# Scores of two heads issued as one group, with the gate products last and the retention scores set apart

## The chip, the cores and the metric

The kernel runs on one core of a Trainium2 chip. The metric is the device time of one launch in microseconds (us); lower is better. Engines are called as the profile calls them: PE is TensorE (matrix products), PEld its weight loads, DVE is VectorE, ACT is ScalarE, POOL is GpSimd, SP is the engine whose queue issues the loads from memory.

## What is computed

Two layers of a decoder over 256 tokens of width 1024. Each layer has a mixer with three groups of heads behind one input projection, then a feed-forward part (dense in the first layer, eight experts of which two are used per token in the second) and a gated embedding. The change touches the mixer alone. Cut to what matters:

```python
def causal_block_attention(q, k, v, scale, cum_logf=None):
    ...
        s = jnp.einsum('bhqd,bhkd->bhqk', q_i, k).astype(jnp.float32) * scale
        if cum_logf is not None:
            s = s + blk[2][..., :, None] - cum_logf[:, :, None, :]
        ...
        w = jax.nn.softmax(s, axis=-1).astype(v.dtype)
        return jnp.einsum('bhqk,bhkv->bhqv', w, v)

def hybrid_mixer(...):
    ...
    o = causal_block_attention(qa, ka, va, HEAD_DIM ** -0.5)
    ...
    o_b = causal_block_attention(split_heads(qb, FOX_HEADS), split_heads(kb, FOX_HEADS),
                                 split_heads(vb, FOX_HEADS), FOX_DIM ** -0.5, cum)
    ...
    o_c = retention_chunkwise(qr, kr, split_heads(vc, RET_HEADS))
```

The first call is differential attention (four pairs of heads), the second forgetting attention (four heads; `cum` is the running sum of the logarithms of the gates, which is added to the scores), the third retention (four heads, scores times a fixed decay). All heads have 64 columns.

## The kernel before, in words

In the mixer each weight block of `w_in` (1 MB) is loaded, split by ACT and DVE into a rounded part `whi` and a rest `wlo` (`Ring.unit`, L178 to L199), and multiplied with the split activations `xh`, `xl` in three products per 128 rows. `tok_chunks` (L313) gives results by token, `col_half` (L344) by column; `col_half` and the VC chunk are 48 products of 128x256 each. Results go through PSUM tiles `mm` (four) and `aux` (four).

Between these blocks stand the small products of the heads:

- `ret_scores(hd)` (L521): two fp32 products of 64 rows, `qkc` with itself, 256 and 128 columns, into one `aux`; DVE multiplies by `c_decay` into `at`.
- `fox_scores(hd)` (L480): `softmax_head` (L353) with `extra`. The queries and keys `qkb` of an even head lie in partitions 0 to 63, of an odd one in 64 to 127. The gates' sums stand in four rows for each head, in partitions from 32 times the head's number on (`row0`, `row1`, written by `fox_rows`, L448). For the first 128 queries and then for the second 128, a 64-row product of `qkb` is followed at once by a 4-row product of the rows, which adds to the same columns:

```python
for a, b, qs, ks in ((0, 128, slice(0, 128), slice(0, 128)), (128, 384, slice(128, 256), slice(0, 256))):
    mm(ps[:, a:b], q[:, qs], k[:, ks], True, extra is None)
    if extra is not None:
        mm(ps[:, a:b], extra[0][:, qs], extra[1][:, ks], False, True)
```

- `diff_scores(p)` (L410): the same helper without `extra`, for the two heads of pair p, on `qa` and `ka`.
- After the scores of a softmax head, DVE adds the mask and takes the row extremes (L363, `nz`, `nm`) and ACT takes the exponentials (L367, `e`).
- `fox_out(hd)` (L488): three transposes of `e` (`turn_w`, L374), a copy to `wt` by ACT (L376), three products with `vb`, and two scalings by DVE (L495). `ret_out()` (L533): twelve products of `at` and `vc`, then a normalisation over `oc` on ACT, DVE and POOL (L538 to L551).

In the trace an fp32 product of the heads leaves two records, one of the gates' rows (rounded type) one.

The order of these calls is written out at the end of `mixer` (L557 to L601); a scheduler of the tile library then places the instructions of each engine, so that blocks overlap a little. Each engine works through its own list in order. Both layers run the same mixer.

Of the kernel before, what the change touches and what calls it, by code (L numbers as in the profile page):

```python
# [11 lines left out]
FT = mybir.dt.float32  # L12
# [3 lines left out]
OP = mybir.AluOpType  # L16
# [19 lines left out]
QA, KA, VA, QB, KB, VB, FB, QC, KC, VC, GC, END = 0, 512, 1024, 1536, 1792, 2048, 2304, 2308, 2564, 2820, 3076, 3332  # L36
# [59 lines left out]
def hymba_trunk(ctx: ExitStack, tc: tile.TileContext, A: dict, out: bass.AP, stop=None, dump=None):  # L96
    nc = tc.nc
    V, G, ACT, PE = nc.vector, nc.gpsimd, nc.scalar, nc.tensor
# [4 lines left out]
    small = pool("small", 4)  # L103
# [3 lines left out]
    def mmtile():  # L107
        return psum.tile([128, 512], FT, name="mm", tag="mm")

    def aux():  # L110
        return psum.tile([128, 512], FT, name="aux", tag="aux")
# [89 lines left out]
    def mm(o, a, b, start, stop):  # L201
        return PE.matmul(o, a, b, start=start, stop=stop, skip_group_check=True)  # L202
# [16 lines left out]
    def tok_mm(o, x, ks, unit, n0, n, t, start, stop):  # L219

        r = slice(t * 128, (t + 1) * 128)
        return steps(o, unit, ks, lambda w, j: w[:, j, n0:n0 + n], x, r, True, start, stop)

    def col_mm(o, x, ks, unit, c0, start, stop):

        steps(o, unit, ks, lambda w, j: w[:, j, c0:c0 + 128], x, slice(0, S), False, start, stop)
# [78 lines left out]
    def mixer(i, ring, xp, xnp, mp, wk, first=None):  # L305
        win = A["w_in"][i]
        g = gain_0 if i == 0 else gain(A["norm_mix"][i])
        x, r = rows_turned(xp, xnp, g)
        r_row = scale_row(r, mp)
        lam_init = 0.8 - 0.6 * math.exp(-0.3 * i)  # L310
        K = {}

        def tok_chunks(*chunks):  # L313
            work = []
            for c0, n, evict in chunks:
                if n > 260:
                    us = [(ring.unit(win[kk * 512:(kk + 1) * 512, c0:c0 + n], 4, n), range(4 * kk, 4 * kk + 4))
                          for kk in range(2)]
                else:
                    src = first if first is not None and c0 == VB else win[:, c0:c0 + n]  # L320
                    us = [(ring.unit(src, 8, n), range(8))]
                work.append((n, evict, us))
                constants(c0)
            for t in range(NT):
                for n, evict, us in work:
                    ps = mmtile()
                    for j, (u, ks) in enumerate(us):
                        tok_mm(ps[:, :n], x, ks, u, 0, n, t, j == 0, j == len(us) - 1)
                    evict(t, ps)
# [14 lines left out]
        def col_half(c0, o, half):  # L344
            u = ring.unit(win[:, c0 + half * 256:c0 + half * 256 + 256], 8, 256)
            for j in range(2):
                ps = mmtile()
                col_mm(ps[:, :S], x, range(8), u, j * 128, True, True)
                V.tensor_tensor(o[:, 2 * half + j], ps[:, :S], r_row, op=OP.mult)

        otok = [xnp.tile([128, D], FT, name="xn", tag="xn") for t in range(NT)]

        def softmax_head(q, k, s, extra=None):  # L353

            ps = aux()
            for a, b, qs, ks in ((0, 128, slice(0, 128), slice(0, 128)), (128, 384, slice(128, 256), slice(0, 256))):
                mm(ps[:, a:b], q[:, qs], k[:, ks], True, extra is None)
                if extra is not None:
                    mm(ps[:, a:b], extra[0][:, qs], extra[1][:, ks], False, True)
            nz = wk.tile([128, 384], FT, name="nz")  # L360
            nm = small.tile([128, 2], FT, name="nm")
            for j, (a, b) in enumerate(((0, 128), (128, 384))):
                V.tensor_tensor_reduce(nz[:, a:b], ps[:, a:b], K["mask"][:, a:b], scale=-0.125, scalar=3e38,  # L363
                                       op0=OP.add, op1=OP.min, accum_out=nm[:, j:j + 1])
            e = wk.tile([128, 384], FT, name="e", bufs=6)
            for j, (a, b) in enumerate(((0, 128), (128, 384))):
                ACT.activation(e[:, a:b], nz[:, a:b], AF.Exp, bias=nm[:, j:j + 1], scale=-1.0,  # L367
                               accum_out=s[:, j:j + 1])
            return e
# [18 lines left out]
        qa = mp.tile([128, 4, S], FT, name="qa")  # L388
        ka = mp.tile([128, 4, S], FT, name="ka")
# [19 lines left out]

        def diff_scores(p):  # L410
            s = small.tile([128, 4], FT, name="ds")
            es = []
            for j in range(2):
                r = slice(64 * j, 64 * j + 64)
                es.append(softmax_head(qa[r, p], ka[r, p], s[:, 2 * j:2 * j + 2]))
            V.reciprocal(s, s)
            V.tensor_scalar(s[:, 2:4], s[:, 2:4], K["nlam"], None, op0=OP.mult)
            w = es[1]
            for j, (a, b) in enumerate(((0, 128), (128, 384))):
                V.tensor_scalar(w[:, a:b], w[:, a:b], s[:, 2 + j:3 + j], None, op0=OP.mult)  # L420
                V.scalar_tensor_tensor(w[:, a:b], es[0][:, a:b], s[:, j:j + 1], w[:, a:b], op0=OP.mult,
                                       op1=OP.add)
            K["w", p] = w
# [18 lines left out]
        qkb = mp.tile([128, 4, S], FT, name="qkb")  # L442
# [34 lines left out]
                V.scalar_tensor_tensor(row, ps[:, :S], K["crow"][:, z:z + 1], rt, op0=OP.add, op1=OP.subtract)  # L477
                K["row", z] = row

        def fox_scores(hd):  # L480
            r = slice(64 * (hd % 2), 64 * (hd % 2) + 64)
            rr = slice(32 * hd, 32 * hd + 4)
            s = small.tile([128, 2], FT, name="fs", bufs=4)
            e = softmax_head(qkb[r, hd // 2], qkb[r, 2 + hd // 2], s, (K["row", 0][rr], K["row", 1][rr]))
            V.reciprocal(s, s)
            K["e", hd] = e, s

        def fox_out(hd):  # L488
            e, s = K.pop(("e", hd))
            wt = turn_w(e)  # L490
            ps = aux()
            o = ps[:, :128].rearrange("p (t n) -> p t n", t=NT)
            av(o, wt, vb, hd * 64, 64)
            for t in range(NT):
                V.tensor_scalar(otok[t][:, 512 + hd * 64:576 + hd * 64], o[:, t], s[:, t:t + 1], None, op0=OP.mult)  # L495
# [3 lines left out]
        vc = mp.tile([128, NT, 256], FT, name="vc")  # L499
# [21 lines left out]
        def ret_scores(hd):  # L521
            dec = K["decay"].rearrange("p (h n) -> p h n", h=4)
            r = slice(64 * (hd % 2), 64 * (hd % 2) + 64)
            q, k = qkc[r, hd // 2], qkc[r, 2 + hd // 2]
            ps = aux()
            mm(ps[:, :256], k[:, :128], q, True, True)
            mm(ps[:, 256:384], k[:, 128:], q[:, 128:], True, True)
            at = wk.tile([128, 384], FT, name="at", bufs=4)
            V.tensor_tensor(at[:, :256], ps[:, :256], dec[:, hd], op=OP.mult)
            V.tensor_tensor(at[:, 256:], ps[:, 256:384], dec[:, hd, :128], op=OP.mult)  # L530
            K["at", hd] = at

        def ret_out():  # L533
            po = aux()
            po_v = po.rearrange("p (t h n) -> p t h n", t=NT, h=4)
            for hd in range(4):
                av(po_v[:, :, hd], K.pop(("at", hd)), vc, hd * 64, 64)
            ACT.copy(oc, po.rearrange("p (g n) -> p g n", n=64))  # L538
            mu = small.tile([128, 8], FT, name="mu", bufs=1)
            V.tensor_reduce(mu, oc, axis=mybir.AxisListType.X, op=OP.add)  # L540
            V.scalar_tensor_tensor(oc, mu[:, :, None].to_broadcast([128, 8, 64]), -1.0 / 64, oc, op0=OP.mult,
                                   op1=OP.add)
            sq = wk.tile([128, 2, 4, 64], FT, name="rot_b", bufs=1).rearrange("p w h d -> p (w h) d")
            ACT.activation(sq, oc, AF.Square)
            va8 = small.tile([128, 8], FT, name="va8", bufs=1)
            V.tensor_reduce(va8, sq, axis=mybir.AxisListType.X, op=OP.add)
            rv = rsqrt_mean(va8, 8, 1.0 / 64)
            V.tensor_tensor(oc, oc, rv[:, :8, None].to_broadcast([128, 8, 64]), op=OP.mult)
            for t in range(NT):
                o = oc[:, 4 * t:4 * t + 4].rearrange("p g n -> p (g n)")  # L550
                V.tensor_tensor(o, o, K["rgn"], op=OP.mult)  # L551
# [6 lines left out]
        tok_chunks((VB, 260, vb_evict), (QC, 512, rotate))  # L558
        fox_rows()
        col_half(QB, qkb, 0)  # L560
        col_half(QB, qkb, 1)
        ret_scores(0)
        ret_scores(1)
        fox_scores(0)
        fox_scores(1)
        tok_chunks((VC, 256, lambda t, ps: V.tensor_scalar(vc[:, t], ps[:, :256], r[t], None, op0=OP.mult)))
        ret_scores(2)
        ret_scores(3)
        fox_scores(2)
        fox_scores(3)  # L570
        col_half(QA, qa, 0)
        fox_out(0)
        fox_out(1)
        ret_out()
        col_half(KA, ka, 0)
        fox_out(2)
        fox_out(3)
        diff_scores(0)
# [658 lines left out]
```

## Time and profile before

| what | value |
|---|---|
| runs | 1496.1, 1492.35 and 1498.77 us, median 1496.1 |
| the profiled execution: its own time | 1499.37 us |
| its span, first to last instruction | 1497.6 us |
| mean granted TensorE clock | 0.988 |
| DVE, ACT busy, share of the span | 80%, 67% |
| loaded from memory | 439.77 MB |

The span lies 1.8 us under the execution's own time. The first layer's mixer runs from the start to about 130 us, the second's from about 365 to 490 us; the experts take most of what follows. A share of busy time is a mean over such stages. Of the clock, 1.00 stands for 2.4 GHz and a fall to 0.5 for 1.2 GHz; a window's clock is a mean over it.

### The profile page before, as it was taken

The numbers are of one execution on the slowest core, as the hardware profiler recorded it, in microseconds if no ns is written. First come the engines' busy times: TensorE is split into PE (matmuls) and PEld (weight loads), VectorE is DVE, ScalarE is ACT, GpSimd is POOL, SyncE is SP. The second block draws the span as 40 slices with busy tenths as digits, with TensorE's granted clock in tenths as the row PEclk, the third lists the DMA queues.
The fourth block names the chain that finished last, engine by engine and source line by source line (L and its number), as shares of the span: only waits on it lengthen the run. The fifth ranks groups of instructions, "written<-read, shape, count | busy, mean of one in ns | idle before, by whom it ended". The sixth has DMA issues, their size and how long they took to land. (4 is left out here: it accounts for less than half of the span.)

```text
span 1497.6 us, 20501 instructions
## 1 busy us (share of the span) xinstructions
PE 1462.2 (98%) x7778; PEld 1228.8 (82%) x7778; DVE 1192.0 (80%) x1209; ACT 1005.1 (67%) x1061; POOL 31.4 (2%) x73
## 2 busy tenths in 40 slices
PE   8999999999999999999999999999999999999997
PEld 7987999997897888887788877888877878888876
DVE  6576555557666687999997999997999998889875
ACT  5455444447546576787976787975787976676756
POOL 0001000001000100000000000000000000000001
PEclk9899999999999999999999999999999999999998
DMA  9634555645624799999998999999999999899940
GB/s 295 174 129 140 182 187 180 196 169 175 205 95 155 275 349 348 355 397 372 407 409 331 378 400 374 403 408 350 379 379 397 397 409 394 317 390 328 387 167 30
DMA packets 166429, 442.25 MB, mean 295 GB/s; under 512 B 13489, under 2 KB 56753, under 8 KB 166322
## 3 DMA queue, kind: packets, MB, share of 16 engines
q1 hardware_dynamic: 166322, 440.85, 79.6%
q8 instruction: 63, 1.03, 0.3%
q14 instruction: 44, 0.36, 0.1%
HBM read 439.77 MB, written 1.05 MB: 294 GB/s over the span
## 5 line engine op out<-in xcount | busy, mean ns | idle before, releaser
L190 DVE TENSOR_TENSOR wlo<-raw,whi 128x2048 fp32r<-128x2048 f32 (+2 forms) x474 | 920.5, 1978 | 146.7 <-ACT whi L189 141.3
L189 ACT CAST whi<-raw 128x2048 fp32r<-128x2048 f32 (+2 forms) x474 | 771.5, 1662 | 254.6 <-PE mm L202 148.3
L202 PE MATMUL mm<-whi,xgh 128*128 128x512 f32 x560 | 222.4, 397 | 0.0
L202 PE MATMUL mm<-whi,xgl 128*128 128x512 f32 x560 | 219.3, 392 | 0.0
L202 PE MATMUL mm<-wlo,xgh 128*128 128x512 f32 x560 | 154.0, 396 | 0.0
L202 PE MATMUL mm<-xh,whi 128*128 128x256 f32 x512 | 131.2, 288 | 0.0
L202 PE MATMUL mm<-xl,whi 128*128 128x256 f32 x512 | 129.9, 286 | 0.0
L202 PEld LDWEIGHTS mm<-whi,xgh 128*128 128x128 f32 x560 | 105.1, 188 | 24.8
L202 PEld LDWEIGHTS mm<-whi,xgl 128*128 128x128 f32 x560 | 105.3, 188 | 22.6
L202 PEld LDWEIGHTS mm<-wlo,xgh 128*128 128x128 f32 x560 | 103.5, 188 | 22.5
L202 PE MATMUL mm<-whi,xh 128*128 128x512 f32 (+2 forms) x328 | 111.6, 355 | 2.3 <-ACT xh L229 2.3
L202 PE MATMUL mm<-whi,xl 128*128 128x512 f32 (+2 forms) x328 | 112.0, 354 | 0.0
L202 PE MATMUL aux<-whi,hxh 128*128 128x512 f32 x280 | 110.4, 396 | 0.7 <-ACT hxh L229 0.7
L202 PE MATMUL aux<-whi,hxl 128*128 128x512 f32 x280 | 109.3, 392 | 0.0
L202 PEld LDWEIGHTS mm<-xh,whi 128*128 128x128 f32 x512 | 98.5, 192 | 1.5 <-issue 0.9
L202 PEld LDWEIGHTS mm<-xl,whi 128*128 128x128 f32 x512 | 98.9, 193 | 0.5
L202 PE MATMUL mm<-wlo,xgp 128*128 128x512 f32 x336 | 95.2, 405 | 1.1
L202 PE MATMUL mm<-whi,xgp 128*128 128x512 f32 x336 | 92.0, 395 | 0.3 <-ACT whi L189 0.2
L202 PE MATMUL mm<-wlo,xh 128*128 128x512 f32 (+2 forms) x328 | 88.8, 351 | 0.1
L202 PE MATMUL mm<-xh,wlo 128*128 128x256 f32 x512 | 83.2, 283 | 0.0
L202 PE MATMUL aux<-wlo,hxh 128*128 128x512 f32 x280 | 77.2, 397 | 0.4 <-DVE wlo L190 0.4
L202 PEld LDWEIGHTS mm<-wlo,xgp 128*128 128x128 f32 x336 | 60.0, 188 | 21.2 <-DVE wlo L190 10.3
(240 smaller groups left out, 1872.4 us busy)
## 6 DMA issues: line engine op xcount, KB each, us to landing
raw<-in_moe_w_gate_dram SPq DMA_DIRECT2D x112, 1024.0 KB, 7.3
raw<-in_moe_w_up_dram SPq DMA_DIRECT2D x112, 1024.0 KB, 7.7
raw<-in_moe_w_down_dram SPq DMA_DIRECT2D x110, 1024.0 KB, 8.0
raw<-in_w_in_dram SPq DMA_DIRECT2D x24, 1024.0 KB, 6.6
raw<-in_dense_w_gate_dram SPq DMA_DIRECT2D x11, 1024.0 KB, 5.4
raw<-in_dense_w_up_dram SPq DMA_DIRECT2D x11, 1024.0 KB, 5.3
raw<-in_dense_w_down_dram SPq DMA_DIRECT2D x11, 1024.0 KB, 5.0
raw<-in_w_out_dram SPq DMA_DIRECT2D x8, 1024.0 KB, 4.9
```

The source lines that it names most:

```text
L189: self.split = (ACT.copy(hi, v[:, k]), V.tensor_tensor(lo, v[:, k], hi.bitcast(FT), op=OP.subtract))
L190: V.tensor_tensor(lo, v[:, k], hi.bitcast(FT), op=OP.subtract))
L202: return PE.matmul(o, a, b, start=start, stop=stop, skip_group_check=True)
```

## The change

`softmax_head` is cut in two. A new `scores_pair` issues the 64-row products of two heads, first both heads' 128 columns and then both heads' 256, and only then, where there are gates, the four 4-row products of both heads. `start` is set on the first part of a tile alone. `fox_scores` now takes a pair of heads, `diff_scores` uses the same helper. The order of the calls changes: the retention's scores no longer stand next to the forgetting ones.

```diff
-        def softmax_head(q, k, s, extra=None):
-
-            ps = aux()
-            for a, b, qs, ks in ((0, 128, slice(0, 128), slice(0, 128)), (128, 384, slice(128, 256), slice(0, 256))):
-                mm(ps[:, a:b], q[:, qs], k[:, ks], True, extra is None)
-                if extra is not None:
-                    mm(ps[:, a:b], extra[0][:, qs], extra[1][:, ks], False, True)
+        PARTS = ((0, 128, slice(0, 128), slice(0, 128)), (128, 384, slice(128, 256), slice(0, 256)))
+
+        def scores_pair(q, k, extra=None):
+
+
+            pss = [aux() for j in range(2)]
+            for n, (a, b, qs, ks) in enumerate(PARTS):
+                for j in range(2):
+                    mm(pss[j][:, a:b], q(j)[:, qs], k(j)[:, ks], n == 0, extra is None)
+            if extra is not None:
+                for a, b, qs, ks in PARTS:
+                    for j in range(2):
+                        mm(pss[j][:, a:b], extra(j)[0][:, qs], extra(j)[1][:, ks], False, True)
+            return pss
+
+        def softmax_head(ps, s):
+
             nz = wk.tile([128, 384], FT, name="nz")
...
         col_half(QB, qkb, 0)
-        col_half(QB, qkb, 1)
         ret_scores(0)
         ret_scores(1)
+        col_half(QB, qkb, 1)
         fox_scores(0)
+        tok_chunks((VC, 256, lambda t, ps: V.tensor_scalar(vc[:, t], ps[:, :256], r[t], None, op0=OP.mult)))
         fox_scores(1)
-        tok_chunks((VC, 256, lambda t, ps: V.tensor_scalar(vc[:, t], ps[:, :256], r[t], None, op0=OP.mult)))
+        col_half(QA, qa, 0)
         ret_scores(2)
         ret_scores(3)
-        fox_scores(2)
-        fox_scores(3)
-        col_half(QA, qa, 0)
         fox_out(0)
         fox_out(1)
+        col_half(KA, ka, 0)
         ret_out()
-        col_half(KA, ka, 0)
         fox_out(2)
         fox_out(3)
         diff_scores(0)
```

On PE, at the first forgetting scores of layer 0, the list before reads as follows (`qkc` are retention products, `qkb` the forgetting heads' 64-row products, `row_379,row_369` the 4-row products of the gates, `mm` a weight block):

```order
L202 MATMUL aux<-qkc 128x256
L202 MATMUL aux<-qkc 128x128
L202 MATMUL aux<-qkc 128x256
L202 MATMUL aux<-qkc 128x128
L202 MATMUL aux<-qkb 128x128
L202 MATMUL aux<-row_379,row_369 128x128
L202 MATMUL aux<-qkb 128x256
L202 MATMUL aux<-row_379,row_369 128x256
L202 MATMUL aux<-qkb 128x128
L202 MATMUL aux<-row_379,row_369 128x128
L202 MATMUL aux<-qkb 128x256
L202 MATMUL aux<-row_379,row_369 128x256
```

And now, at the same scores:

```order
L202 MATMUL mm<-xl,whi 128x256
L202 MATMUL mm<-xh,wlo 128x256 x4
L202 MATMUL aux<-qkb 128x128 x2
L202 MATMUL aux<-qkb 128x256 x2
L202 MATMUL aux<-row_379,row_369 128x128 x2
L202 MATMUL aux<-row_379,row_369 128x256 x2
L202 MATMUL mm<-whi,xh 128x256
```

The seven changes between 64-row and 4-row products within a pair's list have become one, and weight-block products stand on both sides; the retention's four products moved to before the block that precedes these. The number of products is the same.

On ACT, from the end of the QA block to the first two forgetting outputs of layer 0 (`whi` is a weight split, `wt` the copy of the turned weights, `oc` the retention's output), before:

```order
L189 CAST whi<-raw 128x1024
L376 COPY wt<-aux 128x384
L189 CAST whi<-raw 128x1024
L376 COPY wt<-aux 128x384
L538 COPY oc<-aux 128x512
```

And now:

```order
L189 CAST whi<-raw 128x1024 x2
L386 COPY wt<-aux 128x384 x2
L189 CAST whi<-raw 128x1024 x2
L551 COPY oc<-aux 128x512
L386 COPY wt<-aux 128x384 x2
```

The first `wt` now stands behind two weight splits in place of one.

On DVE, from the retention's output to the scores of the first differential pair (`mu`, `va`, `oc` belong to the retention's normalisation, `xn` to the forgetting outputs, `nz,nm` to the differential scores), now:

```order
L553 TENSOR_REDUCE mu<-oc 128x8
L508 TENSOR_SCALAR xn<-aux,fs 128x64
L554 SCALAR_TENSOR_TENSOR oc<-mu,oc 128x512
L508 TENSOR_SCALAR xn<-aux,fs 128x64 x3
L559 TENSOR_REDUCE va_825<-rot_b 128x8
L373 ISA nz,nm<-aux,c_mask 128x128
L373 ISA nm 128x1
L373 ISA nz,nm<-aux,c_mask 128x256
L373 ISA nm 128x1
L561 TENSOR_TENSOR oc<-oc,rs_r 128x512
L373 ISA nz,nm<-aux,c_mask 128x128
```

Before, all the normalisation's instructions up to the products with `rgn` stood ahead of these `xn` and `nz`; now they are mixed with them, and the second head's `nz` stands behind `oc<-oc,rs_r`. The lists of POOL are unchanged, and on SP one load of a gain moved behind one load of weights.

## Rows read from the trace of the kernel before

**Rows 1.** The page: busy us, share of the span and instructions of each engine.

```profile
PE 1462.2 (98%) x7778; PEld 1228.8 (82%) x7778; DVE 1192.0 (80%) x1209; ACT 1005.1 (67%) x1061; POOL 31.4 (2%) x73
```

**Rows 2.** Busy time by stretch, mixer of layer 0: columns in its first line.

```profile
core 0: us, PE busy (x) PEld busy (x) DVE busy (x) ACT busy (x) POOL busy (x), PEclk, DMA share, GB/s
...
37.44:100.00 62.56, 62.43 (x433) 56.59 (x432) 38.82 (x109) 26.49 (x56) 1.85 (x2) 0.92 0.49 148
```

**Rows 3.** Waits of SP's queue from 500 us on: us in total, times, longest.

```profile
SPq L123 <- DVE wlo L190: 681.8, 304, 8.4
```

**Rows 4.** Timeline of PE, first forgetting scores, layer 0: start us, us, instruction.

```profile
42.90 0.63 PE L202 MATMUL mm<-xh,wlo 128*128 128x256 f32 x4
43.46 0.93 PE L202 MATMUL aux<-qkc 64*128 64x256 f32 x8
44.22 0.38 PE L202 MATMUL aux<-qkb 64*128 64x128 f32 x2
44.53 0.32 PE L202 MATMUL aux<-row,row 4*128 4x128 f32 x1
44.79 0.70 PE L202 MATMUL aux<-qkb 64*128 64x256 f32 x2
45.41 0.38 PE L202 MATMUL aux<-row,row 4*128 4x256 f32 x1
...
47.02 0.38 PE L202 MATMUL aux<-row,row 4*128 4x256 f32 x1
47.33 0.39 PE L202 MATMUL mm<-whi,xh 128*128 128x256 f32 x1
```

**Rows 5.** Timeline of PE, last forgetting outputs and first differential scores, layer 0.

```profile
78.27 0.49 PE L374 MATMUL aux<-ident,e 128*128 128x128 f32 x3
...
82.17 0.93 PE L202 MATMUL aux<-ka,qa 64*128 64x128 f32 x8
83.03 0.39 PE L202 MATMUL mm<-xh,wlo 128*128 128x256 f32 x1
```

**Rows 6.** Busy time by stretch around the forgetting scores of both layers.

```profile
47.30:51.20 3.90, 3.90 (x21) 3.88 (x21) 1.92 (x7) 1.38 (x6) 0.00 (x0) 0.57 0.52 150
...
55.50:58.90 3.40, 3.40 (x16) 1.89 (x12) 2.78 (x9) 1.79 (x5) 0.00 (x0) 0.88 0.00 0
58.90:65.00 6.10, 6.10 (x29) 6.09 (x29) 2.46 (x9) 1.04 (x5) 0.00 (x0) 0.51 0.52 153
...
403.10:406.20 3.10, 3.10 (x16) 1.82 (x13) 2.82 (x9) 2.77 (x5) 0.00 (x0) 1.00 0.18 67
406.20:409.70 3.50, 3.50 (x17) 3.48 (x17) 1.92 (x7) 1.38 (x6) 0.00 (x0) 0.51 0.17 16
...
414.40:417.50 3.10, 3.10 (x16) 1.82 (x12) 2.81 (x9) 1.49 (x4) 0.00 (x0) 1.00 0.00 0
417.50:423.00 5.50, 5.50 (x47) 5.48 (x47) 2.35 (x8) 1.37 (x6) 0.00 (x0) 1.00 0.46 127
```

**Rows 7.** Timeline of ACT, first forgetting output, layer 0.

```profile
67.15 1.05 ACT L189 CAST whi<-raw 128x1024 fp32r<-128x1024 f32 x1 [6.81 <-issue]
68.10 0.47 ACT L376 COPY wt<-aux 128x384 f32<-128x384 f32 x1
```

**Rows 8.** Timeline of PE, first forgetting output, layer 0.

```profile
67.37 0.49 PE L374 MATMUL aux<-ident,e 128*128 128x128 f32 x3
...
68.63 0.88 PE L202 MATMUL aux<-vb,wt 128*128 128x64 f32 x6
```

**Rows 9.** Timeline of DVE, the retention's normalisation, layer 0; in brackets the idle time before.

```profile
74.64 0.69 DVE L540 TENSOR_REDUCE mu<-oc 128x8 f32<-128x512 f32 x1 [2.82 <-ACT oc L538]
...
79.49 0.69 DVE L548 TENSOR_TENSOR oc<-oc,rs_r 128x512 f32<-128x512 f32 x1 [2.06 <-POOL rs_r L238]
80.21 0.76 DVE L551 TENSOR_TENSOR oc<-oc,rgn 128x256 f32<-128x256 f32 x2
```

**Rows 10.** Busy time by stretch, from the last forgetting outputs on, layer 0.

```profile
80.00:90.00 10.00, 9.97 (x84) 8.91 (x83) 9.20 (x30) 4.88 (x13) 0.00 (x0) 1.00 0.31 105
90.00:100.00 10.00, 10.00 (x63) 8.97 (x62) 6.41 (x17) 3.75 (x10) 0.00 (x0) 1.00 0.41 140
```

More of the change, by code (lines that the diff above doesn't have):

```diff
@@ L411, in diff_scores @@
             s = small.tile([128, 4], FT, name="ds")
[L412 to L415, printed above, removed]
+            r = [slice(64 * j, 64 * j + 64) for j in range(2)]
+            pss = scores_pair(lambda j: qa[r[j], p], lambda j: ka[r[j], p])
+            es = [softmax_head(pss[j], s[:, 2 * j:2 * j + 2]) for j in range(2)]
             V.reciprocal(s, s)
@@ L478, in fox_rows, with fox_scores @@
                 K["row", z] = row
[L480 to L486, printed above, removed]
+        def fox_scores(p):
+            r = [slice(64 * j, 64 * j + 64) for j in range(2)]
+            rr = [slice(32 * (2 * p + j), 32 * (2 * p + j) + 4) for j in range(2)]
+            pss = scores_pair(lambda j: qkb[r[j], p], lambda j: qkb[r[j], 2 + p],
+                              lambda j: (K["row", 0][rr[j]], K["row", 1][rr[j]]))
+            for j in range(2):
+                s = small.tile([128, 2], FT, name="fs", bufs=4)
+                e = softmax_head(pss[j], s)
+                V.reciprocal(s, s)
+                K["e", 2 * p + j] = e, s
         def fox_out(hd):
```

## The prediction

> **What bounds the kernel now.** I read the page first: PE is busy for 98% of the span [rows 1]. That alone says little, because matmuls overlap, so the stage that the change touches is read next. In the mixer of layer 0, PE is busy for 62.43 of 62.56 us while DVE, ACT and the DMA have large reserves [rows 2]. The mixer is bound by PE: what PE saves there, the stage saves, as long as nobody is late for it. The same view shows a granted clock of 0.92 in this stretch, which is the second thing to look at. The experts that follow are paced by SP's queue, which waits for a raw buffer that DVE's split gives back (681.8 us over 304 waits [rows 3]). Their loads start when the second mixer and the routing behind it are through, so an earlier mixer moves that stage as a whole. I take a microsecond of PE in either mixer as a microsecond of the run.
>
> **The forgetting scores.** There are four groups of a retention pair and a forgetting pair, two in each layer. The timeline of PE shows one: the retention pair starts at 43.46 us, the first weight-block product after the group at 47.33, so 3.87 us. A block product comes every 0.117 us (47 of them in 5.50 us [rows 6]); four that start at 42.90 end their turns at 43.37, so entering the group costs another 0.09. A group costs 3.96 us [rows 4].
>
> What is slow in it? The two 64-row products of one forgetting head take 0.31 us (44.22 to 44.53) and 0.62 (44.79 to 45.41), 0.93 for a head. The two heads of a differential pair, with the same columns, take 0.86 together, and this holds their way back to the block products (82.17 to 83.03 [rows 5]). So two heads in different halves of the partitions run side by side when nothing stands between them, and the gates' rows stop that. Each 4-row product holds the queue by itself: 0.26 us for 128 columns (44.53 to 44.79), 0.31 for 256 (47.02 to 47.33), though a full block product of 256 columns needs 0.117.
>
> After the change the retention pair stands alone: 0.09 in and 0.86 (it has the differential pair's columns), 0.95. The forgetting pair costs 0.09 in, 0.86 for both heads up to the point where another kind of product starts, and x for the four 4-row products with the way back. The trace has no such run of 4-row products, so x is bounded: it cannot be under the last one's own 0.31, and if each of the four still holds the queue by itself it is 2 x (0.26 + 0.31) = 1.14. I take 0.43, one return of 0.31 and one product of at most 0.12, because the heads of a pair lie in different strips again and the differential heads, the nearest row, do not stop for each other. That is 0.95 + 1.38 = 2.33 us a group, 1.63 less than now, and 6.5 us in four groups; the bounds are 7.0 (x = 0.31) and 3.7 (x = 1.14).
>
> The Trainium skill has a rule for this (TensorEngine Tiling, section Key Properties): a change of the tiling mode drains the engine, a change of the tile within a mode does not. By it the 4-row products of two heads would not stop for each other, and x would be at the lower of the two values; the differential heads agree, and no run here shows it for 4-row products.
>
> **The clock.** After three of the four groups the granted clock falls to the lower level, 1.2 GHz. In each case PE had been busy without a gap, but with the small products: 3.10 of 3.10 us at clock 1.00 in layer 1, then 0.51 for the next 3.50 us [rows 6]. What it costs is read from the same rows as time x (1 - clock): 3.90 x 0.43 = 1.68, then 3.40 x 0.12 = 0.41 and 6.10 x 0.49 = 2.99 at the second group, 3.50 x 0.49 = 1.72 in layer 1. That is 6.8 us. After the fourth group, with the same 16 records in 3.10 us, it did not fall (5.50 us at 1.00), so a group stands near the edge. Shorter groups of 0.95 and 1.38 us, each between blocks of 48 products (5.6 us), should stay clear of it; the forgetting outputs and the two differential pairs between 80 and 90 us are such small products, and there the clock is 1.00 [rows 10]. I count all 6.8 as gained; the bounds are 0 and 6.8.
>
> **What moves.** *ACT* splits two halves of weights ahead of the first `wt`, before it was one. A split takes 0.95 us until the next instruction starts (67.15 to 68.10), so `wt` ends at 67.15 + 1.90 + 0.47 = 69.5 [rows 7] and the product with `vb` starts about 2.2 us after the QA block ended at 67.37; before it was 1.26 [rows 8]. The retention pair that now stands in between takes 0.95 of this, counted above. What is left over is one block product fewer as filling, 0.12, so I charge 0.1 a layer, 0.2 in all; bounds 0 and 1.9, which is the whole split of 0.95 in each layer.
>
> *The retention scores of heads 0 and 1* come a block earlier, directly behind the gates' sums; their queries were there long before. *`ret_out`* comes a block later, next to the last two forgetting outputs and the first differential scores. Its normalisation runs from 74.64 to 80.97 us on DVE with a wait of 2.06 us for POOL in the middle [rows 9], 6.3 us that a block of KA covered. Now only the two outputs and the pair of scores cover it, 78.27 to 83.03 [rows 5], and the start is 0.85 us behind `ret_out`'s end, so DVE is late by 0.85 + 6.3 - 4.8 = 2.4 us with the second head's mask. DVE has 10.00 - 6.41 = 3.59 us idle in the next stretch [rows 10] and PE has a QA block to work on, so I cost this at nothing; if the cover is gone, it is the last rival. The swap of two loads on SP costs nothing: the weights it brings are used a block and more later, and the DMA works half its time there [rows 2].
>
> **The sum.** 6.5 + 6.8 - 0.2 = 13.1 us. Against the profiled execution's own 1499.4 us that gives 1486.3. This execution lies 3.3 us above the median of the runs, 1496.1, against which it would give 1483.0. I cannot tell whether the median run lost as much to the clock, so I take the middle, 1484.5.
>
> **Rivals.**
>
> 1. *The clock is not the scores' doing, or falls elsewhere instead.* Then only 6.5 - 0.2 = 6.3 us are gained: 1493.1 from the profiled execution, 1489.8 from the median. For it: the fourth group kept its clock with the same products, so they alone do not decide; `ret_out`, two forgetting outputs and the differential scores now stand in one row of small products. Against it: the falls come only after these groups in the two mixers. The Trainium skill (TensorE: Matmul & The Clock Gate, table of the two states in Part 1) puts the lower clock down to an engine that was idle; by this rule busy scores would not lower it and this rival would hold. The trace differs: PE was busy all the time before each fall. Chance 0.25.
>
> 2. *The 4-row products still hold the queue one by one* (the grouping does not do what it is for): 3.7 + 6.8 - 0.2 = 10.3, so 1489.1 or 1485.8. For it: nothing in the trace shows two of them side by side. Against it: the heads of 64 rows do. Chance 0.12.
>
> 3. *DVE becomes late for PE, and the run slower.* The place is the end of `ret_out` in each layer: DVE waits for POOL, the second differential head's mask and the QA results stand behind it in DVE's list, and PE comes to stand for want of a free tile. The price is at most the 6.3 us of the chain in each layer and a fall of the clock behind each stop, 1.72 as in layer 1: 2 x (6.3 + 1.7) = 16.0, against 13.1 saved: 1502.3. It decides once DVE's delay is over its 3.59 us of reserve, and I expect 2.4. Chance 0.03.
>
> The forecast itself keeps 0.60.
>
> **How the numbers follow.** A measurement of this kernel can tell about 0.5%, 7.5 us: faster is under 1488.6, slower over 1503.6. The forecast lies under this line but for its last few runs (0.57 of 0.60), rival 2 mostly (0.08 of 0.12), rival 1 hardly (0.04 of 0.25); rival 3 is slower by more only at its worst. So 0.69 faster, 0.28 the same, 0.03 slower. The range starts at 1480: the best bounds, 7.0 + 6.8 = 13.8 us, from the median, and 2 to 3 us for the spread of runs. It ends at 1491.5, between the two values of rival 1.
>
> **What would show it.** In the changed profile PE should go from the first `qkb` product to the next block product in about 1.3 us (wrong if over 1.8), the retention pairs in 0.86. The clock should be 1.00 through both mixers (wrong if there is a stretch at 0.5 behind a forgetting or retention pair, or behind `ret_out`). PE's idle time before `vb` products and differential scores should not grow by over 0.5 us a layer. The experts should start about 13 us earlier and take as long as before; if the mixers end earlier and the run does not, the premise on the experts is wrong.

## The result, and the profile after

| | before | changed |
|---|---|---|
| median | 1496.51 us | 1485.94 us |
| range, 8 runs each | 1492.35 to 1499.39 | 1483.68 to 1490.03 |
| the profiled execution, its own time | 1499.37 us | 1484.13 us |
| its span | 1497.6 us | 1482.4 us |
| mean granted clock | 0.988 | 0.996 |

The ratio of the times is 0.9933, with a 95% interval of 0.9920 to 0.9947. The changed kernel is 10.6 us faster by the medians, 15.2 by the two profiled executions; the prediction was 1484.5, with a range of 1480.0 to 1491.5.

The page of the changed kernel, the row that answers to [rows 1]:

```profile
PE 1445.4 (98%) x7778; PEld 1214.0 (82%) x7778; DVE 1191.5 (80%) x1209; ACT 1005.0 (68%) x1061; POOL 31.6 (2%) x73
```

The same number of products takes 16.8 us less of PE and 14.8 us less of its weight loads; DVE, ACT and POOL are as they were. The timeline of PE shows where (start, us, instruction, as in [rows 4, 5]):

```profile
37.74 0.93 PE L202 MATMUL aux<-qkc 64*128 64x256 f32 x8
38.60 0.38 PE L202 MATMUL mm<-xl,whi 128*128 128x256 f32 x1
...
44.38 0.93 PE L202 MATMUL aux<-qkb 64*128 64x128 f32 x8
45.24 0.49 PE L202 MATMUL aux<-row,row 4*128 4x128 f32 x4
45.66 0.39 PE L202 MATMUL mm<-whi,xh 128*128 128x256 f32 x1
...
74.40 0.93 PE L202 MATMUL aux<-ka,qa 64*128 64x128 f32 x8
```

The retention pair takes 37.74 to 38.60 = 0.86 us. The forgetting pair takes 44.38 to 45.66 = 1.28, of which the run of 4-row products and the way back are 0.42. All four forgetting pairs of the program give 1.28. The first differential pair starts at 74.40, before at 82.17 [rows 5]. (A 64-row product leaves two records, so x8 is four products; a 4-row product leaves one.)

The clock, by busy time in stretches (columns as in [rows 2]). First the mixer of layer 0, then the weight blocks behind the four forgetting pairs:

```profile
37.00:100.00 63.00, 62.84 (x478) 56.56 (x476) 42.96 (x115) 31.98 (x63) 1.85 (x2) 1.00 0.54 167
```

```profile
45.66:51.55 5.89, 5.89 (x51) 5.75 (x49) 3.64 (x13) 2.60 (x10) 0.00 (x0) 1.00 0.91 309
52.83:58.73 5.90, 5.90 (x51) 5.76 (x49) 3.70 (x14) 2.53 (x10) 0.00 (x0) 1.00 0.85 177
397.07:402.99 5.92, 5.92 (x50) 5.78 (x48) 3.66 (x13) 3.87 (x11) 0.00 (x0) 1.00 0.67 224
404.27:410.17 5.90, 5.90 (x51) 5.76 (x49) 3.59 (x13) 2.58 (x10) 0.00 (x0) 1.00 0.51 156
```

The clock is 1.00 in all four and the blocks take 5.89 to 5.92 us, where [rows 6] showed 0.57, 0.51 and 0.51. The same four blocks in the kernel before, each from its first product to the start of what follows it:

```profile
47.33:54.73 7.40, 7.40 (x49) 7.27 (x49) 2.40 (x8) 1.72 (x7) 0.00 (x0) 0.77 0.76 209
58.91:67.37 8.46, 8.46 (x49) 8.46 (x49) 2.46 (x9) 1.25 (x6) 0.00 (x0) 0.64 0.49 126
406.22:413.66 7.44, 7.44 (x49) 7.30 (x49) 2.40 (x8) 1.73 (x7) 0.00 (x0) 0.77 0.46 143
417.52:423.43 5.91, 5.91 (x51) 5.91 (x51) 2.35 (x8) 1.73 (x7) 0.00 (x0) 1.00 0.50 145
```

Three of them hold a fall of the clock and take 7.40, 8.46 and 7.44 us; the fourth, at 1.00, takes 5.91.

The table measures the mixers in every kernel of this study by the starts of rows of PE. "Scores" runs from the first gate product (`c_tri`) to the first differential pair, "end" from the last differential pair to the first product of what follows (in layer 0 the dense layer's down projection, in layer 1 the router). What lies between the differential pairs is the same in all.

| kernel | scores, layer 0 | end, layer 0 | scores, layer 1 | end, layer 1 | sum, us |
|---|---|---|---|---|---|
| before | 45.72 | 63.54 | 42.84 | 36.99 | 189.10 |
| before_again | 42.74 | 63.53 | 42.85 | 36.79 | 185.91 |
| changed | 38.09 | 64.00 | 38.16 | 37.44 | 177.68 |
| after_again | 38.10 | 64.00 | 38.17 | 37.43 | 177.69 |
| apart_only | 43.43 | 63.57 | 45.00 | 37.01 | 189.01 |
| grouped_only | 37.40 | 64.02 | 37.50 | 37.43 | 176.36 |
| diff_by_head | 38.09 | 63.58 | 38.17 | 37.01 | 176.85 |
| grouped_diff_by_head | 37.39 | 63.50 | 37.49 | 36.98 | 175.36 |
| rows_by_part | 38.78 | 63.96 | 38.86 | 37.44 | 179.04 |
| scores_four_times | 42.02 | 63.98 | 42.10 | 37.22 | 185.32 |
| one_head_five_times | 43.31 | 63.95 | 43.39 | 37.44 | 188.10 |

Of the 15.2 us between the two spans, 11.4 lie in the mixers. The rest, 3.8, lies where the change does nothing: 0.4 before and between the mixers, 2.6 in the experts (956.6 to 954.0 us, from the router's first product to the last product with the tile `pt`), 0.8 behind them.

In the experts this difference goes with the clock, too. The kernel before has a granted clock of 0.83 in three stretches of 10 us there (510 to 520, 680 to 690, 910 to 920 us), the changed one in one (670 to 680), a second profile of the changed one (after_again) in two, with 955.2 us. Over all eleven profiles the experts take 954.0 us with one such fall (six profiles), 955.2 to 955.5 with two (three) and 956.4 to 956.6 with three (the two of the kernel before). Since one kernel had one fall and then two, the profiles do not tell whether the change has a part in this.

The experts are still paced as in [rows 3], here in SP's waits from 490 us on:

```profile
SPq L123 <- DVE wlo L190: 673.0, 303, 8.4
```

### The profile page after: what moved, and what is told of

Its sections match the earlier page's. It is cut to its first block, busy times and chain, and to the rows that moved or that the text cites. A ratio compares the mean times of both kernels' runs of the same rounds, so it can differ in the third digit from the quotient of the medians.

```text
span 1482.4 us, 20502 instructions
## 1 busy us (share of the span) xinstructions
PE 1445.4 (98%) x7778; PEld 1214.0 (82%) x7778; DVE 1191.5 (80%) x1209; ACT 1005.0 (68%) x1061; POOL 31.6 (2%) x73
```

## The experiments

Three questions were open after this. Which part of the change gives the time: the grouping of the products, or the new places of the calls? Why does the end of each mixer take 0.45 us more than before? And what lowers the clock behind the old groups, their small products or the changes of kind? (The kind of a product is here its number of rows, 64 or 4.)

### The grouping alone, in the old places (grouped_only)

The changed kernel, with the calls in the order of before:

```diff
         col_half(QB, qkb, 0)
+        col_half(QB, qkb, 1)
         ret_scores(0)
         ret_scores(1)
-        col_half(QB, qkb, 1)
         fox_scores(0)
...
+        ret_scores(2)
+        ret_scores(3)
         fox_scores(1)
         col_half(QA, qa, 0)
-        ret_scores(2)
-        ret_scores(3)
```

(`ret_out` is also back ahead of the KA block.)

> The new grouping of products with the old order of the calls: retention pair and forgetting pair stand together again. Both theories: a group takes about 0.76 + 0.86 + 0.42 = 2.04 us from the first retention product to the next block product, against 3.87 before, so four groups save 7.3 us, less the 0.9 us that both mixers' ends lose (PE stands 1.22 in place of 0.75 us before the GC products). Theory A (a long run of small products is what lowers the clock; 2.0 us is too short for it): no fall to 0.5 behind the groups, another 5.9 us, in all about 1484.2 us against 1496.5 before, level with the changed kernel. Theory B (standing next to the retention scores is enough, the grouping alone does not help the clock): two or three falls of about 3.5 us stay, 1490 us.

Measured: 1483.04 us median of 6 runs (1481.45 to 1487.09), ratio to before 0.9922, interval 0.9903 to 0.9940. The timeline of PE, first group of layer 0:

```profile
45.68 0.93 PE L202 MATMUL aux<-qkc 64*128 64x256 f32 x8
46.44 0.83 PE L202 MATMUL aux<-qkb 64*128 64x128 f32 x8
47.20 0.49 PE L202 MATMUL aux<-row,row 4*128 4x128 f32 x4
47.62 0.39 PE L202 MATMUL mm<-whi,xh 128*128 128x256 f32 x1
```

Both pairs together take 45.68 to 47.62 = 1.94 us, less than the 0.86 + 1.28 = 2.14 of the changed kernel, since PE goes once less from the block products to the 64-row ones and back. Busy time of the blocks behind both groups of layer 0:

```profile
47.62:53.52 5.90, 5.90 (x50) 5.76 (x48) 4.02 (x17) 2.23 (x9) 0.00 (x0) 1.00 0.73 244
55.47:61.26 5.79, 5.79 (x50) 5.79 (x49) 3.99 (x17) 2.09 (x9) 0.00 (x0) 1.00 0.74 136
```

The clock stays at 1.00 although the two pairs stand next to each other. The grouping gives the whole gain, and the new places are not needed: the mixers end 1.3 us earlier without them (177.68 - 176.36).

### The new places alone, with the old products (apart_only)

The kernel before, with the calls where the changed one has them:

```diff
         col_half(QB, qkb, 0)
-        col_half(QB, qkb, 1)
         ret_scores(0)
         ret_scores(1)
+        col_half(QB, qkb, 1)
         fox_scores(0)
...
-        ret_scores(2)
-        ret_scores(3)
         fox_scores(2)
         fox_scores(3)
         col_half(QA, qa, 0)
+        ret_scores(2)
+        ret_scores(3)
```

(`ret_out` also moves behind the KA block.)

> The new order of the calls with the old products, head by head with the gates' rows in between. A group costs an entry and a way back more (0.2 us each, 0.8 in all). Theory A1 (only the whole run of 3.87 us is long enough to lower the clock): no falls, 5.9 us gained, 0.8 lost, about 1491.4 us. Theory A2 (the forgetting pair's 3.1 us with the 4-row products is enough by itself): falls stay behind some of the four pairs, 1495 to 1498 us. Theory B (the neighbourhood of retention scores lowers the clock): as A1.

Measured: 1498.97 us median of 12 runs, ratio to before 1.0017, interval 1.0004 to 1.0030. Busy time of the first forgetting pair and the block behind it, of the blocks behind the second and third, and of the fourth pair and its block:

```profile
46.75:49.95 3.20, 3.20 (x13) 1.90 (x13) 2.20 (x6) 2.62 (x6) 0.00 (x0) 1.00 0.87 272
49.95:55.84 5.89, 5.89 (x49) 5.76 (x48) 2.40 (x8) 1.35 (x5) 0.00 (x0) 1.00 0.79 268
...
59.17:66.42 7.25, 7.25 (x49) 7.12 (x48) 2.46 (x9) 1.30 (x5) 0.00 (x0) 0.79 0.58 147
...
406.32:413.72 7.40, 7.40 (x49) 7.26 (x49) 2.40 (x8) 1.97 (x9) 0.00 (x0) 0.77 0.46 144
413.72:416.92 3.20, 3.20 (x13) 1.90 (x12) 2.26 (x6) 2.61 (x6) 0.00 (x0) 1.00 0.00 0
416.92:424.32 7.40, 7.40 (x49) 7.26 (x48) 2.34 (x8) 1.34 (x5) 0.00 (x0) 0.77 0.46 142
```

PE is busy for 3.20 of 3.20 us in the first pair and in the fourth; behind the first the clock stays, behind the other three it falls: 7.25 to 7.40 us for a block that takes 5.89 without a fall. Moving the retention scores away does not protect the clock. By itself the new order is worth nothing, or 2.5 us less than nothing.

### The differential scores head by head (diff_by_head)

The changed kernel, with the differential heads' products issued one head at a time, each followed by its softmax:

```diff
-            pss = scores_pair(lambda j: qa[r[j], p], lambda j: ka[r[j], p])
-            es = [softmax_head(pss[j], s[:, 2 * j:2 * j + 2]) for j in range(2)]
+            for j in range(2):
+                ps = aux()
+                for n, (a, b, qs, ks) in enumerate(PARTS):
+                    mm(ps[:, a:b], qa[r, p][:, qs], ka[r, p][:, ks], n == 0, True)
+                es.append(softmax_head(ps, s[:, 2 * j:2 * j + 2]))
```

> The changed kernel, but the differential scores are issued head by head as before. Theory: at the end of the mixer the pairwise issue made the scheduler put a scaling that waits for POOL ahead of the last head's mask on DVE, so the exponentials, the table load for the gate and the next products came 0.47 us later in each layer; head by head, PE stands 0.75 us there again and the run is 0.9 us shorter than the changed kernel, about 1485.0 us. The scores themselves stay at 0.86 us a pair. Rival: the wait comes from the earlier arrival of the stage, then PE stands 1.2 us as in the changed kernel and the time is the same, 1485.9.

This asks for the 0.45 us at the end of each mixer. There PE waits for ACT ahead of the first products of the mixer's output projection (128x512; two of the expectations call them the GC products, but those have 256 columns and are done by then). Before, by PE's timeline:

```profile
117.73 0.50 PE L202 MATMUL mm<-whi,xh 128*128 128x512 f32 x1 [0.75 <-ACT xh L229]
```

and in the changed kernel:

```profile
110.39 0.97 PE L202 MATMUL mm<-whi,xh 128*128 128x512 f32 x3 [1.22 <-ACT xh L229]
```

Its timeline of DVE shows what comes ahead of that (`nz` masks the last differential heads, `xn` scales the output of the pair before them):

```profile
103.77 0.35 DVE L445 SCALAR_TENSOR_TENSOR xn<-aux,rs_r,sub 128x128 f32<-128x128 f32 x1 [0.67 <-POOL rs_r L238]
...
105.41 0.28 DVE L373 CUSTOM_DVE_ANT_0 nz<-aux,c_mask 128x128 f32<-128x128 f32 x1
105.62 0.42 DVE L373 CUSTOM_DVE_ANT_0 nz<-aux,c_mask 128x256 f32<-128x256 f32 x1
```

The same place in the kernel before:

```profile
112.12 0.60 DVE L436 SCALAR_TENSOR_TENSOR xn<-aux,rs_r,sub 128x128 f32<-128x128 f32 x2
112.64 0.41 DVE L363 CUSTOM_DVE_ANT_0 nz<-aux,c_mask 128x256 f32<-128x256 f32 x1
```

The changed kernel's timeline of ACT shows what follows:

```profile
106.14 0.49 ACT L377 ACTIVATE e<-nz,nm 128x256 f32<-128x256 f32 x1
...
107.00 1.28 ACT L567 ACT_TABLE_LOAD   x1
```

DVE now waits 0.67 us for POOL with both parts of the last head's mask behind it. Before, the first part came at 110.79, and only the second stood behind the scaling `xn`, which did not wait. Counted from the last differential pair (108.96 before, 101.19 now), the last exponential starts after 4.95 us instead of 4.51, and the table load of 1.28 us for the gates is later by 0.43. The split `xh` that PE waits for stands behind these on ACT.

Measured with the scores head by head: 1485.81 us median of 6 runs, ratio to before 0.9935 (0.9917 to 0.9953). The wait in PE's timeline:

```profile
112.14 0.98 PE L202 MATMUL mm<-whi,xh 128*128 128x512 f32 x3 [0.76 <-ACT xh L229]
```

The wait is 0.76 us again, and the mixers' ends are 0.42 and 0.43 us shorter, as in the kernel before. So the pairwise issue of the differential scores costs 0.85 us in the two layers together and brings nothing, since their products take 0.86 a pair either way [rows 5]. In the whole time this is too little for these runs to tell.

### The 4-row products behind each part (rows_by_part)

The changed kernel, with the gates' products directly behind both heads' 128 columns and again behind both heads' 256, so that the kind changes three times within a pair, not once (the cuts in the lines are marked by dots):

```diff
             for n, (a, b, qs, ks) in enumerate(PARTS):
                 for j in range(2):
                     mm(pss[j][:, a:b], q(j)[:, qs], ...
-            if extra is not None:
-                for a, b, qs, ks in PARTS:
+                if extra is not None:
                     for j in range(2):
                         mm(pss[j][:, a:b], extra(j)[0][:, qs], ...
```

> The changed kernel, but the 4-row products of both heads follow each part (128 columns, rows, 256 columns, rows): two heads still stand side by side, and the queue changes between 64-row and 4-row products three times a pair in place of once. Theory (each change between the two kinds costs, about 0.2 us): a pair takes 1.28 + 2 x 0.2 = 1.7 us. Rival (what cost time was that the heads could not stand side by side): 1.3 us as now.

Measured: 1486.85 us in one run. The timeline of PE, first pair:

```profile
45.49 0.49 PE L202 MATMUL aux<-qkb 64*128 64x128 f32 x4
45.91 0.33 PE L202 MATMUL aux<-row,row 4*128 4x128 f32 x2
46.17 0.70 PE L202 MATMUL aux<-qkb 64*128 64x256 f32 x4
46.80 0.39 PE L202 MATMUL aux<-row,row 4*128 4x256 f32 x2
47.12 0.39 PE L202 MATMUL mm<-whi,xh 128*128 128x256 f32 x1
```

The pair takes 45.49 to 47.12 = 1.63 us instead of 1.28, with the same products. Two more changes of kind cost 0.35, so 0.17 each. The table's scores are 0.69 us longer in layer 0, twice that. So a change of kind has a price of its own, with the products and the heads' pairing kept.

### The best of the parts together (grouped_diff_by_head)

The grouped products in the old places, with the differential scores head by head (the two edits above together).

> The grouping for the forgetting heads alone: old order of the calls, differential scores head by head. Theory (the grouping is worth 1.92 us a group and the falls of the clock, the new order costs 0.3 us a group in entries and ways back, the pairwise differential scores cost 0.45 us a layer): 1.5 us shorter than the changed kernel from the order and 0.9 from the end of the mixer, about 2.3 us, 1483.5 us where the changed kernel has 1485.9. No fall of the clock in the mixers, PE stands 0.75 us before the GC products. Rival (what grouped_only gained over the changed kernel was chance of its runs): no difference.

Measured: 1483.71 us median of 6 runs (1481.85 to 1485.61), ratio to before 0.9925 (0.9904 to 0.9947). The changed kernel, run once more (after_again):

> The changed kernel once more on this chip, for the comparison with the grouping alone, and to see the clock in a second profile. Theory (the groups are too short to lower the clock): again 1.00 through both mixers, 1486 us. Rival (the first profile had luck): a fall of 3.5 us behind one of the pairs, 1.5 us each.

It gave 1487.86 us median of 9 runs (1482.87 to 1489.92), 0.9939 (0.9920 to 0.9959), and mixers equal to the first profile's within 0.01 us, at clock 1.00. The mixers of the best version are 2.3 us shorter (177.69 - 175.36), in every one of the four stretches. In the whole time the medians stand in the same order, but the intervals overlap.

### Long runs of small products without changes (scores_four_times, one_head_five_times)

The clock fell behind groups of some 3 us of small products. It could be their small use of PE that does it, or the changes of kind. The first kernel issues the 64-row products of a forgetting pair four times, and the 4-row ones once:

```diff
-            for n, (a, b, qs, ks) in enumerate(PARTS):
-                for j in range(2):
+            for again in range(4 if extra is not None else 1):
+                for n, (a, b, qs, ks) in enumerate(PARTS):
+                    for j in range(2):
```

> The changed kernel, but the 64-row products of the forgetting pair are issued four times over (each time from anew, so the result is the same) before the gates' rows follow once. A pair then takes 1.28 + 3 x 0.64 = 3.2 us, as long as the old forgetting pair of 3.11 us, side by side and without any further change between 64-row and 4-row products. Theory L (the length of the run of small products lowers the clock): falls to 0.5 behind two to four of the four pairs, 7.7 us for the products and 1.5 a fall. Theory D (the waiting at the changes between the two kinds, eight in the old pair, lowers it): 1.00 through both mixers, 7.7 us longer than the changed kernel.

Measured: 1495.83 us in one run, beside 1495.35 for the kernel before in the same comparison. The pair takes 3.24 us, as long as the old groups' forgetting part. Busy time of the pairs and the blocks behind them, all four:

```profile
46.28:55.42 9.14, 9.14 (x85) 8.41 (x84) 4.80 (x14) 3.86 (x11) 0.00 (x0) 1.00 0.91 288
55.42:64.50 9.08, 9.08 (x85) 8.41 (x84) 4.74 (x15) 3.75 (x11) 0.00 (x0) 1.00 0.45 78
401.60:410.77 9.17, 9.17 (x85) 8.45 (x84) 4.80 (x14) 5.14 (x12) 0.00 (x0) 1.00 0.62 216
410.77:420.00 9.23, 9.23 (x87) 8.50 (x86) 4.80 (x14) 3.95 (x11) 0.00 (x0) 1.00 0.39 115
```

No fall. But two heads side by side use both halves of PE's rows, and an old group used one half at a time. So the second kernel repeats the two products of head 0 alone, four times ahead of the normal ones:

```diff
+            for again in range(4 if extra is not None else 0):
+                for n, (a, b, qs, ks) in enumerate(PARTS):
+                    mm(pss[0][:, a:b], q(0)[:, qs], k(0)[:, ks], n == 0, False)
```

> The changed kernel, but the 64-row products of the even head of each forgetting pair are issued five times over (each time from anew), those of the odd head once: a run of about 1.28 + 4 x 0.64 = 3.8 us in which mostly one half of the partitions is in use, and still only one change between 64-row and 4-row products. Theory D (the waiting at the changes lowers the clock): 1.00 through both mixers, 10.2 us longer than the changed kernel, about 1496 us. Theory H (a head working alone, with half of the array, lowers it): falls behind two to four of the pairs, up to 6 us more, about 1502 us.

Measured: 1496.55 us, beside 1497.03 for the kernel before, one run each. The pair takes 3.89 us; busy time of the first pair with its block, and of the last:

```profile
44.73:54.51 9.78, 9.78 (x78) 8.97 (x77) 4.80 (x14) 3.87 (x11) 0.00 (x0) 1.00 0.95 280
...
411.64:421.00 9.36, 9.36 (x75) 8.70 (x75) 4.80 (x14) 3.49 (x10) 0.00 (x0) 1.00 0.37 112
```

Again no fall, in the two pairs between them neither. Long runs of small products, with one half of the rows or with both, leave the clock at 1.00. What is left of the differences between these pairs and the old ones is the alternation between 64-row and 4-row products, and with it that the old pairs do fewer products in the same time.

### The kernel before, once more (before_again)

> The kernel before once more, to count the falls of the clock in a second profile. The first had three, behind the first and second group of layer 0 and the first of layer 1, worth 5.9 us by the lengths of the blocks behind them. Theory (whether a group lowers the clock is chance): another number of falls, two to four, at other groups. Rival (it is fixed by the program): the same three.

Measured: 1495.84 us. Busy time of the blocks behind its four groups:

```profile
47.36:54.76 7.40, 7.40 (x49) 7.27 (x49) 2.40 (x8) 1.72 (x7) 0.00 (x0) 0.77 0.80 224
58.62:64.42 5.80, 5.80 (x50) 5.80 (x49) 2.46 (x9) 1.58 (x7) 0.00 (x0) 1.00 0.50 140
403.01:408.94 5.93, 5.93 (x49) 5.79 (x49) 2.40 (x8) 1.74 (x7) 0.00 (x0) 1.00 0.49 145
412.80:420.13 7.33, 7.33 (x50) 7.33 (x50) 2.34 (x8) 1.62 (x7) 0.00 (x0) 0.77 0.47 144
```

Two falls, behind the first and the fourth group; [rows 6] had three, behind the first, second and third. So the program alone does not fix which group is hit, and no run shows what does. Over the profiles with the old products the clock fell behind 8 of 12 forgetting pairs (before 3, here 2, apart_only 3), over the other eight profiles behind 0 of 32. Of these 32, the eight repeated ones are the test; the others are short (1.19 to 1.63 us) as well as grouped, so that no fall behind them tells nothing of the cause.

## Why the prediction was right, point by point

**Switching: 6.5 us forecast, 6.6 measured.** A group was 3.96 us and is now 0.09 + 0.86 + 0.09 + 1.28 = 2.32, so 1.64 less, four times. The value that was chosen between far bounds, x = 0.43 for the run of 4-row products, measures 0.42. Rival 2, in which they hold PE one by one (x = 1.14), is out: of all four products the start of the next kind is 0.42 us away, where two of them took 0.57 before. The tiling rule of the Trainium skill (TensorEngine Tiling, section Key Properties) put x near its lower bound, and the traces agree: where only the tile within a kind changes there is no stop, and rows_by_part shows 0.17 us for a change of kind. An estimate of what makes up the 1.83 us by which a forgetting pair is shorter (3.11 to 1.28): six changes of kind fewer at 0.17 are 1.0, and four 64-row products at 0.163 instead of 0.326 us (last section) are 0.65.

**The clock: 6.8 us forecast, 5.9 measured.** The falls are gone, as forecast, and rival 1 is false: the clock is 1.00 through both mixers in two profiles of the changed kernel. The term was mis-sized. By the lengths of the blocks, 7.40 - 5.89 = 1.51 behind the first group; at the second 8.46 - 5.90 and 0.31 more in the pair itself, 2.87; 7.44 - 5.92 = 1.52 in layer 1. The step that failed is "time x (1 - clock)", which takes half of the time at the lower level as lost. The timeline of PE before shows block products at the lower level and, from 64.84 us on, at the higher one:

```profile
62.92 0.41 PE L202 MATMUL mm<-xh,whi 128*128 128x256 f32 x1
63.13 0.41 PE L202 MATMUL mm<-xl,whi 128*128 128x256 f32 x1
...
65.12 0.28 PE L202 MATMUL mm<-xl,whi 128*128 128x256 f32 x1
65.24 0.28 PE L202 MATMUL mm<-xh,whi 128*128 128x256 f32 x1
```

They start 0.21 us apart at the lower level and 0.12 at the higher, 1.8 times, not twice. So 0.09 of 0.21 us is lost, 0.44 of the time instead of half, which is 0.9 of the term; at the first group 0.9 x 1.68 is the measured 1.51. Lengths of equal blocks need no such assumption.

**The cause of the falls** was put too wide. "A group stands near the edge", with shorter groups between blocks to stay clear of it, gave the right forecast partly by luck: scores_four_times and one_head_five_times show that the length of a run of small products is not enough, and grouped_only that the neighbouring retention scores are not. What the falls in the mixers followed is alternation between 64 and 4 rows. Whether the changes of kind themselves do it, or what PE leaves undone while it waits at them, no run tells apart. The trace still differs from the rule in the Trainium skill (TensorE: Matmul & The Clock Gate, table of the two states in Part 1), which puts the lower clock down to an idle engine: in the records PE is busy for 3.20 of 3.20 us before the last fall in the mixers of apart_only. The records cannot show whether it stands still within a product's time, so a rule about idleness could yet hold on a finer scale. In the experts, which the prediction did not look at for this, falls did come behind true idleness: PE waits three times for DVE there, 2.0 us each (to 682.86, 913.52 and 1144.26 us in the kernel before, to 669.94, 900.70 and 1129.88 in the changed one); the clock fell at the first two in the kernel before and at the first in the changed one.

**ACT: 0.2 us forecast.** From the end of the QA block to the first product with `vb` it is now 58.73 to 60.84 = 2.11 us, forecast about 2.2. Five block products fill it, six before, so the charge of 0.12 a layer was of the right size.

**DVE: costed at nothing.** At the place that the prediction named, the two differential pairs start 5.44 us apart (74.40 and 79.84), exactly as before (82.17 and 87.61), so the delay behind `ret_out` was covered and rival 3 did not come. But a delay of the same kind, DVE waiting for POOL ahead of a mask, came at another place, the end of the mixer, and cost 0.45 us a layer. The prediction had looked at the order on DVE around `ret_out` alone; the pairwise issue changed it at every differential pair.

**The sum.** 6.6 + 5.9 - 0.9 - 0.2 = 11.4, which is what the mixers lost (189.10 - 177.68). Two terms were a little too good, 0.9 each, and so 13.1 was forecast. The profiled executions differ by more, 15.2, through the 3.8 us elsewhere, which mostly go with falls of the clock in the experts that the prediction had not counted.

**The choice of the middle between the profile and the median.** The doubt whether a median run lost as much to the clock was in place: before_again, with two falls, has mixers 8.2 us longer than the changed kernel's, the first profile, with three, 11.4. The medians are 10.6 apart, between the two. The forecast of 1484.5 lies 1.4 us under the median. That it lies so near is in part luck: the sum was 1.7 us too large, and the middle was taken for want of knowledge. **The premise on the experts**, that an earlier mixer moves them as a whole, held: the router's first product came 11.9 us earlier (501.89 to 490.04), and the experts took 954.0 us, not longer than before.

## What to carry to other kernels

Issue small products by their number of rows, all of one kind together and for two heads at once, so that PE changes its kind once in a group; the cost of a change is read as the distance to the next start, since the records show PE as busy across it. Look at the lengths of equal blocks behind a suspicious group, not only at the group: there a fall of the clock is paid, mostly 1.5 us here behind a group of 3 us that is hit. Try such a change in its parts, for here one of three parts gave all of the gain and the other two took 2.3 us of it back, one through the order of work on DVE at a place far from the edit.

## What the runs showed of the hardware that was not expected

The granted clock fell behind 8 of 12 pairs whose 64-row and 4-row products alternate, with PE shown as busy throughout, and behind none of the 32 other pairs, of which eight ran as long (3.24 and 3.89 us). In two profiles of the same kernel it fell behind different groups, so a single profile tells that a group is at risk, not that it will be hit.

Two heads in different halves of the rows really run side by side: the 12 additional products of scores_four_times, spread over both heads, cost 3.24 - 1.28 = 1.96 us, 0.163 each; the 8 additional ones of one head alone cost 3.89 - 1.28 = 2.61, 0.326 each, exactly twice as much.
